# Split weights kept as single runs of 512 columns, and the first gate and up steps taken by halves

## The chip, the cores and the metric

The kernel runs on one core of a Trainium2 chip. The time is the device time of one execution in microseconds, as the median of several runs. One execution was also recorded by the hardware profiler; its page and trace are what is quoted as "the profile" and "the trace". In them PE is TensorE (matmuls), PEld its weight loads, DVE is VectorE, ACT is ScalarE, POOL is GpSimd and SP is SyncE, which here issues nearly all DMAs.

## What is computed

A two-layer encoder on a sequence of 256 rows of 1024 values. Each layer has a mixer with three groups of heads (neighbourhood attention, dilated window attention, grouped-query attention) and a gated feed-forward block. Weights and activations are float32.

```
def mixer_sublayer(x, ...):
    h = rms_norm(x, n1)
    proj = h @ w_in_l                       # 1024 x 2560
    ...                                     # three kinds of attention
    return x + mix @ w_out_l                # 1024 x 1024

def channel_sublayer(x, n2, w_gu, cw, cb, w_dn):
    h = rms_norm(x, n2)
    g, u = jnp.split(h @ w_gu, 2, axis=-1)  # 1024 x 5632
    g = depthwise_conv_centred(g, cw, cb)   # three taps along the rows
    return x + (jax.nn.gelu(g, approximate=False) * u) @ w_dn   # 2816 x 1024

for l in range(DEPTH):                      # DEPTH = 2
    x = mixer_sublayer(x, ...)
    x = channel_sublayer(x, ...)
```

The input is one batch of 256 x 1024 values; `D_FF` is 2816.

## The kernel before

**Split weights.** PE multiplies in fp32r. To keep float32 accuracy each weight and each activation is split into a high part (ACT casts it to fp32r, tile `wp_hi`) and a low part (DVE subtracts the high part from the original, tile `wp_lo`). Products of the two operands are then summed in up to three matmuls (`mm3`, line 595; in the gate and up steps two, since the activation's two parts lie side by side and go through one matmul of 512 columns).

**Units.** Weights are taken in units of at most 2048 columns (8 KB a partition), listed by `units_of` (line 530) in the order of use: twelve units of the input projections, six of the output projections (three or two chunks of 512), and for the feed-forward block `FFN` (line 69): G0, U0, G1, D0, U1, G2, D1, U2 and so on, where G, U and D are steps of gate, up and down. A gate or up unit is 8 input chunks by 256 columns, a down unit 2 chunks by 1024 columns. `load` (line 547) issues a unit's DMA into one of four raw buffers (tile `wp_raw`). `split` (line 569) makes the unit's two parts in places for two units: tags `hi` and `lo`, each a tile of 2048 columns in `PARTS` = 2 buffers. It works in pieces of about 512 columns, for a down unit 1024. A place comes free when the last matmul that reads the unit is done. `unit` (line 584) gives out the next unit; before that it puts into the program the loads up to four units and the splits up to `AHEAD` = 2 units, the one given out among them.

**The order of the work.** The program isn't issued as written. `Plan` (line 217) first collects all operations with their dependences, and `order` (line 298) lists them out by a cost model: of all operations that could start on their engines it takes the one with the earliest start, and among equal ones the one with the lowest rank. The rank is the place in the program, raised for some: the splits and loads by `SPLIT_LATER` = 50. Places of one tag are given in the order in which their tiles are first used in the program (`t.turn != s.given`), even where a later tile could use one sooner. So the place of a split in the program sets its rank and its turn, not its time.

**The passage from mixer to feed-forward block.** In lines 1206 to 1210 the last two output-projection units add to x; `split_T` (line 608) transposes half of x (input chunks 0 to 3) on PE and makes its high and low part (`h2`, in the trace `act_hT`) on ACT and DVE. `half_up` (line 1219) is a gate or up step: for each of two column groups j and each chunk k one matmul of 512 and one of 256 columns, 32 in all, into two banks of the pool `psw`. The first gate step takes chunks 0 to 3 of both groups, then makes the other half of `h2` with `split_T`, then takes chunks 4 to 7, and ends with `row_scale`.

`gate` (line 1264) copies and adds the two halves of each bank (`joined`, ACT and DVE), scales, applies the three taps (ACT, then DVE), and takes the gelu on ACT. `up` (line 1283) joins its banks, multiplies by the gelu's result and splits that into `act_ch` and `act_cl`. `down` (line 1293) multiplies these with a down unit into four banks `dacc` of the pool `psa`, which it holds through the block. The tiles of `joined`, of the taps and of the gelu share the tag `s2k` with five places.

The helper that issues every operation is line 402, so every row of the profile names line 402, and the rows are told apart by their tiles: `wp_hi`, `wp_lo` (split weights), `act_hT` (the normalised input), `psw` and `psa` (accumulators), `act_s2k` (gate and softmax work), `const_x` (x).

Of the kernel before, what the change touches and what calls it, by code (L numbers as in the profile page):

```python
# [11 lines left out]
F32 = mybir.dt.float32  # L12
# [6 lines left out]
P = 128  # L19
# [21 lines left out]

RAWS, PARTS, AHEAD, CHUNK = 4, 2, 2, 512

# [401 lines left out]
def encoder_kernel(  # L445
# [101 lines left out]
    def load(i):  # L547
# [19 lines left out]
        raws.append(raw)  # L567

    def split(i):
        v = views[i]  # L570
        a, b = v.shape[1], v.shape[2]
        n = a * b
        raw = raws[i]
        hi = wp.tile([P, UNIT], F32R, tag="hi", name=f"hi{i}", bufs=PARTS)
        lo = wp.tile([P, UNIT], F32R, tag="lo", name=f"lo{i}", bufs=PARTS)
        h = b if i < 2 else b * max(1, CHUNK // b)
        for c in range(0, n, h):
            e = min(c + h, n)
            nc.scalar.copy(hi[:, c:e], raw[:, c:e])
            nc.vector.tensor_tensor(lo[:, c:e], raw[:, c:e], hi[:, c:e].bitcast(F32), op=ALU.subtract)  # L580
        r = lambda z: z[:, :n].rearrange("p (a b) -> p a b", b=b)
        parts.append((r(hi), r(lo)))

    def unit():

        i = taken[0]
        taken[0] += 1
        with nc.later(SPLIT_LATER):
            while len(raws) < min(i + AHEAD + RAWS - PARTS, len(views)):
                load(len(raws))  # L590
            while len(parts) < min(i + AHEAD, len(views)):
                split(len(parts))
        return parts[i]
# [181 lines left out]
    for l in range(DEPTH):  # L775
# [9 lines left out]
        pj = {}  # L785

        def projections():
            for (c0, width), name in zip(PROJ, PROJ_NAMES):
                ps = [psa.tile([P, 512], F32, tag="a", name=f"pj_{name}{l}{t}") for t in range(NT)]
                per = 4 if width * 8 > UNIT else 8  # L790
                for k0 in range(0, KD, per):
                    wh, wl = unit()
                    for t in range(NT):
                        c = slice(t * P, (t + 1) * P)
                        for k in range(per):
                            kk = k0 + k
                            mm3(
                                ps[t][:, :width], hT_hi[:, kk, c], hT_lo[:, kk, c],
                                wh[:, k], wl[:, k], kk == 0, kk == KD - 1,
                            )  # L800
                            yield 3 * width / 2.4
                pj[name] = ps
                yield name
# [7 lines left out]
        def out_projections(order):  # L811
            for gi, h in order:
                k0, n = OUTP[gi]
                yield ("wait", f"mix{gi}")
                wh, wl = unit()
                for t in range(NT):
                    c = slice(t * P, (t + 1) * P)
                    ps = psa.tile([P, 512], F32, tag="a", name=f"po{gi}_{l}{t}_{h}")
                    for k in range(n):
                        kk = k0 + k  # L820
                        mm3(
                            ps, mixT_hi[:, kk, c], mixT_lo[:, kk, c], wh[:, k], wl[:, k], k == 0, k == n - 1
                        )
                        yield 3 * 512 / 2.4
# [393 lines left out]

        def half_up(name, first=False):

            wh, wl = unit()
            ps = [psw.tile([P, 2, S], F32, tag="w", name=f"{name}{j}") for j in range(2)]

            def part(j, k):
                js = slice(j * P, (j + 1) * P)
                nc.tensor.matmul(ps[j], wh[:, k, js], h2[:, k], start=k == 0, stop=False)
                nc.tensor.matmul(ps[j][:, 0], wl[:, k, js], h2_hi[:, k], start=False, stop=k == KD - 1)

            if first:
                for k in range(4):  # L1230
                    part(0, k)
                for k in range(4):
                    part(1, k)
                split_T(halves(1), h2_hi, h2_lo, 4, gains[:, 2, l, 4:8], f"n2{l}1")
                for k in range(4, KD):
                    part(0, k)
                for k in range(4, KD):
                    part(1, k)
                row_scale()
                return ps  # L1240
# [52 lines left out]
        def down(steps):  # L1293
            ws = [unit() for _ in steps]
            for h in range(2):
                hs = slice(h * 512, (h + 1) * 512)
                for t in range(NT):
                    c = slice(t * P, (t + 1) * P)
                    for s, (wh, wl) in zip(steps, ws):
                        ch, cl = ready[s]  # L1300
                        for j in range(2):
                            mm3(
                                dacc[t][h], ch[:, j, c], cl[:, j, c], wh[:, j, hs], wl[:, j, hs],
                                s == 0 and j == 0, s == STEPS - 1 and j == 1,
# [99 lines left out]
```

## Time and profile before

| | |
|---|---|
| median of 3 runs | 617.96 us (617.42 to 618.77) |
| the profiled execution | 618.73 us |
| its span, first to last instruction | 616.9 us |
| granted TensorE clock | 1.000 |
| DVE busy | 487.1 us (79%) |
| ACT busy | 429.8 us (70%) |
| HBM read | 102.54 MB |

A row of a timeline has the start from the span's beginning, the duration, the engine, the line, the operation, the tile written and the tiles read, the shapes, the count of merged instructions, and in brackets the idle time of the engine before it and what ended that. A row of a group has the count, the busy time, the mean of one in ns, and the idle time before. A row of stretches has start and end, then the busy time of each engine. Matmuls are pipelined and their ends are modelled, so a busy PE isn't PE at its peak.

### The profile page before, as it was taken

The page shows a single profiled execution, that of the slowest core. Times are in us where ns is not written, and L with a number is a line of the kernel's source. Part 1 is how long each engine was busy: PE and PEld are TensorE (multiplying, and loading weights), DVE is VectorE, ACT ScalarE, POOL GpSimd, SP SyncE. Part 2 cuts the span into 40 slices and gives each one's busy share as a digit, 9 for nine tenths or more (in the row PEclk, how much of TensorE's full clock was granted, in tenths as well). Part 3 has the DMA queues.
Part 4 walks back from the last instruction along what each step waited for, and adds up shares of the span by engine and source line. Part 5 has one row for each costly group of instructions (what it writes and reads, how often), then busy time and mean ns, then how long its engine had stood idle before and what let it go on. Part 6 is the DMA issues. An engine that isn't in the chain of part 4 may idle for free.

```text
span 616.9 us, 9838 instructions
## 1 busy us (share of the span) xinstructions
PE 607.5 (98%) x3496; PEld 525.4 (85%) x3496; DVE 487.1 (79%) x1000; ACT 429.8 (70%) x1064; POOL 78.1 (13%) x125
## 2 busy tenths in 40 slices
PE   8999999999999999999999999999999999999997
PEld 6998888878888888888899989887888888888885
DVE  4898888897878777777867798979877777787775
ACT  6888898777565565556588899897756566556651
POOL 2732130111600000000023212112000000000000
PEclk9999999999999999999999999999999999999999
DMA  8894303466596566554444632127575565556501
GB/s 276 270 285 163 104 34 105 143 218 198 195 225 224 176 201 204 198 169 162 154 147 151 232 104 86 35 73 247 181 236 172 188 206 192 166 189 203 178 29 68
DMA packets 81345, 104.66 MB, mean 170 GB/s; under 512 B 9464, under 2 KB 68952, under 8 KB 81296
## 3 DMA queue, kind: packets, MB, share of 16 engines
q1 hardware_dynamic: 80720, 103.51, 52.0%
q8 instruction: 27, 0.44, 0.3%
q10 hardware_dynamic: 576, 0.53, 0.3%
q14 instruction: 22, 0.18, 0.1%
HBM read 102.54 MB, written 1.49 MB: 169 GB/s over the span
## 4 chain that ended last, share of the span: by engine, by line
PE 93%; ACT 3%; DVE 2%; DMA 1%; issue 1%; ACTq 0%
PE psw_w L402 49%; PE psa_a L402 44%; ACT act_s2k L402 2%; DMA const_x<-in_x_dram 1%; DVE wp_lo L402 1%; DVE act_hT L402 1%; ACT act_ch L402 0%; DVE const_x L402 0%; ACTq L402 0%; ACT wp_hi L402 0%; DVE small_nm L402 0%; ACT act_mixT_hi L402 0%; DVE act_z L402 0%; ACT act_sqm L402 0%; DVE small_rs L402 0%
## 5 line engine op out<-in xcount | busy, mean ns | idle before, releaser
L402 DVE TENSOR_TENSOR wp_lo<-wp_raw,wp_hi 128x512 fp32r<-128x512 f32 (+2 forms) x348 | 244.5, 732 | 48.2 <-ACT wp_hi L402 46.3
L402 PE MATMUL psw_w<-act_hT,wp_hi 128*128 128x512 f32 x704 | 247.8, 397 | 2.7 <-DVE act_hT L402 2.7
L402 ACT CAST wp_hi<-wp_raw 128x512 fp32r<-128x512 f32 (+2 forms) x348 | 213.0, 659 | 25.0 <-PE psw_w L402 15.7
L402 PE MATMUL psw_w<-act_hT,wp_lo 128*128 128x256 f32 x704 | 195.8, 279 | 0.0
L402 PEld LDWEIGHTS psw_w<-act_hT,wp_hi 128*128 128x128 f32 x704 | 131.9, 188 | 35.1 <-DVE act_hT L402 3.9
L402 PEld LDWEIGHTS psw_w<-act_hT,wp_lo 128*128 128x128 f32 x704 | 132.6, 188 | 1.1
L402 PE MATMUL psa_a<-wp_hi,act_hT 128*128 128x384 f32 (+2 forms) x448 | 113.4, 333 | 0.0
L402 ACT COPY act_s2k<-psw_w 128x256 f32<-128x256 f32 x88 | 32.4, 373 | 80.5 <-PE psw_w L402 80.5
L402 PEld LDWEIGHTS psa_a<-wp_hi,act_hT 128*128 128x128 f32 x448 | 78.7, 190 | 2.4
L402 PE MATMUL psa_a<-wp_lo,act_hT 128*128 128x384 f32 (+2 forms) x224 | 75.0, 335 | 0.0
L402 PE MATMUL psa_a<-wp_lo,act_ch 128*128 128x512 f32 x176 | 69.5, 395 | 0.0
L402 PE MATMUL psa_a<-wp_hi,act_ch 128*128 128x512 f32 x176 | 69.3, 394 | 0.0
L402 PE MATMUL psa_a<-wp_hi,act_cl 128*128 128x512 f32 x176 | 66.1, 394 | 0.0
L402 DVE TENSOR_TENSOR act_s2k<-psw_w,act_s2k 128x256 f32<-128x256 f32 x88 | 36.8, 422 | 30.6 <-ACT act_s2k L402 30.2
L402 PEld LDWEIGHTS psa_a<-wp_lo,act_hT 128*128 128x128 f32 x224 | 42.4, 189 | 2.0 <-DVE wp_lo L402 1.1
L402 PEld LDWEIGHTS psa_a<-wp_hi,act_cl 128*128 128x128 f32 x176 | 33.1, 188 | 7.8
L402 PEld LDWEIGHTS psa_a<-wp_hi,act_ch 128*128 128x128 f32 x176 | 33.1, 188 | 7.8
L402 PEld LDWEIGHTS psa_a<-wp_lo,act_ch 128*128 128x128 f32 x176 | 33.1, 188 | 6.9
L402 DVE SCALAR_TENSOR_TENSOR act_s2k<-act_s2k,act_cw,act_s2k 128x255 f32<-128x255 f32 x88 | 36.8, 478 | 1.4 <-ACT act_s2k L402 1.3
L402 ACT ACTIVATE act_s2k<-act_s2k,act_cw 128x256 f32<-128x256 f32 x44 | 24.1, 595 | 11.6 <-DVE act_s2k L402 11.6
L402 POOL TENSOR_TENSOR small_rstd<-small_ms,const_mh 128x6 f32<-128x6 f32 (+2 forms) x26 | 31.5, 1210 | 2.1
L402 ACT ACTIVATE act_s2k<-act_s2k 128x512 f32<-128x512 f32 x22 | 13.9, 632 | 22.4 <-DVE act_s2k L402 22.4
(109 smaller groups left out, 773.3 us busy)
## 6 DMA issues: line engine op xcount, KB each, us to landing
wp_raw<-in_w_gate_up_dram SPq DMA_DIRECT2D x44, 1024.0 KB, 5.0
wp_raw<-in_w_down_dram SPq DMA_DIRECT2D x22, 1024.0 KB, 4.9
wp_raw<-in_w_in_dram SPq DMA_DIRECT2D x14, 768.0 KB, 5.7
wp_raw<-in_w_in_dram SPq DMA_DIRECT2D x8, 1024.0 KB, 5.8
wp_raw<-in_w_out_dram SPq DMA_DIRECT2D x8, 768.0 KB, 4.3
wp_raw<-in_w_out_dram SPq DMA_DIRECT2D x4, 512.0 KB, 3.7
act_nab<-dram_scr SPq DMA_DIRECT2D x4, 448.0 KB, 7.1
out_dram<-const_x SPq DMA_DIRECT2D x4, 256.0 KB, 2.0
```

Of the source, the lines that this page charges most:

```text
L402: getattr(o.engine.real, o.method)(*map(real, o.args), **{k: real(v) for k, v in o.kw.items()})
```

## The change

A unit's parts are no longer one tile of 2048 columns but single runs of at most 512, each with a place of its own: eight places a part (`PIECES`), as many bytes as before. `grain` says how a unit is cut: projections as before; a down unit into four runs (chunk by half of the columns) instead of two of 1024; a gate or up unit into four runs of four chunks by 128 columns, one column group at a time, instead of four runs of two chunks by 256. `AHEAD` becomes 3, so a split stands in the program one unit earlier; the loads stay at four units. The order of the matmuls in the projections and in all later steps stays as it was (`by_rows` is defined and not used).

`first_halves` joins the first gate step and the first up step of each layer: chunks 0 to 3 of G0, the other half of `h2`, chunks 0 to 3 of U0, chunks 4 to 7 of G0, `row_scale`, chunks 4 to 7 of U0. U0's two banks come from the pool `psa` there.

```diff
-RAWS, PARTS, AHEAD, CHUNK = 4, 2, 2, 512
+RAWS, PIECES, LOAD_AHEAD, AHEAD, CHUNK = 4, 8, 4, 3, 512
...
+    PER_LAYER = len(views) // DEPTH
+
+    def grain(i, a, b):
+
+        if b > CHUNK:
+            return 1, CHUNK
+        if i % PER_LAYER >= PER_LAYER - len(FFN):
+            return 4, P
+        return max(1, CHUNK // b), b
+
     def split(i):
         v = views[i]
         a, b = v.shape[1], v.shape[2]
         n = a * b
         raw = raws[i]
-        hi = wp.tile([P, UNIT], F32R, tag="hi", name=f"hi{i}", bufs=PARTS)
-        lo = wp.tile([P, UNIT], F32R, tag="lo", name=f"lo{i}", bufs=PARTS)
-        h = b if i < 2 else b * max(1, CHUNK // b)
-        for c in range(0, n, h):
-            e = min(c + h, n)
-            nc.scalar.copy(hi[:, c:e], raw[:, c:e])
-            nc.vector.tensor_tensor(lo[:, c:e], raw[:, c:e], hi[:, c:e].bitcast(F32), op=ALU.subtract)
-        r = lambda z: z[:, :n].rearrange("p (a b) -> p a b", b=b)
-        parts.append((r(hi), r(lo)))
+        rv = raw[:, :n].rearrange("p (a b) -> p a b", b=b)
+
+        per, w = (1, b) if i < 2 else grain(i, a, b)
+        cuts = [(k, c) for c in range(0, b, w) for k in range(0, a, per)]
+        both = {}
+        for k, c in cuts:
+            pair = [wp.tile([P, per, w], F32R, tag=g, name=f"{g}{i}_{k}_{c}", bufs=PIECES) for g in ("hi", "lo")]
+            src = rv[:, k : k + per, c : c + w]
+            nc.scalar.copy(pair[0], src)
+            nc.vector.tensor_tensor(pair[1], src, pair[0].bitcast(F32), op=ALU.subtract)
+            both[k // per, c // w] = pair
+        parts.append(lambda k, c=0, n=b: [z[:, k % per, c % w : c % w + n] for z in both[k // per, c // w]])
 
     def unit():
 ...
-            while len(raws) < min(i + AHEAD + RAWS - PARTS, len(views)):
+            while len(raws) < min(i + LOAD_AHEAD, len(views)):
                 load(len(raws))
             while len(parts) < min(i + AHEAD, len(views)):
                 split(len(parts))
...
-        def half_up(name, first=False):
...
+        def products(ps, w, j, ks):
+
+            for k in ks:
+                wh, wl = w(k, j * P, P)
+                nc.tensor.matmul(ps[j], wh, h2[:, k], start=k == 0, stop=False)
+                nc.tensor.matmul(ps[j][:, 0], wl, h2_hi[:, k], start=False, stop=k == KD - 1)
...
+        def half_up(name):
+            ps, w = banks(psw, "w", name), unit()
             for j in range(2):
-                for k in range(KD):
-                    part(j, k)
+                products(ps, w, j, range(KD))
             return ps
+
+        def first_halves():
+
+            G, U = banks(psw, "w", f"G{l}_0"), banks(psa, "a", f"U{l}_0")
+            wg = unit()
+            for j in range(2):
+                products(G, wg, j, range(4))
+            split_T(halves(1), h2_hi, h2_lo, 4, gains[:, 2, l, 4:8], f"n2{l}1")
+            wu = unit()
+            for j in range(2):
+                products(U, wu, j, range(4))
+            for j in range(2):
+                products(G, wg, j, range(4, KD))
+            row_scale()
+            for j in range(2):
+                products(U, wu, j, range(4, KD))
+            return G, U
...
         def gate(s):
             nm = f"{l}_{s}"
-            Gs = joined(half_up(f"G{nm}", s == 0), f"Gs{nm}")
+            if s == 0:
+                hold["G"], hold["U"] = first_halves()
+            Gs = joined(hold["G"] if s == 0 else half_up(f"G{nm}"), f"Gs{nm}")
...
         def up(s):
             nm = f"{l}_{s}"
-            C = joined(half_up(f"U{nm}"), f"C{nm}")
+            C = joined(hold["U"] if s == 0 else half_up(f"U{nm}"), f"C{nm}")
```

Elsewhere a unit's parts are taken by a call, `w(k)` or `w(j, h * 512, 512)`, where they were slices of one tile.

More of the change, by code (lines that the diff above doesn't have):

```diff
@@ L785, in encoder_kernel, with by_tiles, by_rows @@
         pj = {}
+        def by_tiles(n):
+            return [(t, k) for t in range(NT) for k in range(n)]
+        def by_rows(n):
+            return [(t, k) for k in range(n) for t in range(NT)]
         def projections():
@@ L1298, in down @@
                     c = slice(t * P, (t + 1) * P)
-                    for s, (wh, wl) in zip(steps, ws):
+                    for s, w in zip(steps, ws):
                         ch, cl = ready[s]
```

40 lines of the change are left out of this document (10 added, 30 removed).

## The prediction

> **What bounds the kernel now.** I read the page first: the span, the engines' busy time, and the idle time ahead of the feed-forward matmuls.
>
> ```profile
> span 616.9 us, 9838 instructions
> ...
> PE 607.5 (98%) x3496; PEld 525.4 (85%) x3496; DVE 487.1 (79%) x1000; ACT 429.8 (70%) x1064; POOL 78.1 (13%) x125
> ...
> L402 PE MATMUL psw_w<-act_hT,wp_hi 128*128 128x512 f32 x704 | 247.8, 397 | 2.7 <-DVE act_hT L402 2.7
> ```
>
> PE is busy for 607.5 of 616.9 us. The change adds and removes no matmul, so it can only move the 9.4 us in which PE is idle. 2.7 us of these stand in one group: gate and up matmuls that wait for the normalised input (act_hT). Then I cut the span into stretches of the first layer.
>
> ```profile
> core 0: us, PE busy (x) PEld busy (x) DVE busy (x) ACT busy (x) POOL busy (x), PEclk, DMA share, GB/s
> 100.60:114.30 13.70, 13.55 (x90) 11.27 (x88) 9.86 (x31) 13.63 (x38) 1.69 (x4) 1.00 0.24 81
> 124.10:130.50 6.40, 5.07 (x31) 4.31 (x31) 6.40 (x14) 5.96 (x15) 2.15 (x3) 1.00 0.63 223
> 130.50:143.80 13.30, 13.30 (x79) 11.69 (x79) 10.91 (x21) 9.79 (x17) 0.00 (x0) 1.00 0.54 183
> 233.27:249.94 16.67, 16.67 (x90) 14.23 (x89) 12.52 (x22) 9.97 (x19) 0.00 (x0) 1.00 0.56 188
> ```
>
> The last row is one steady step of gate, up and down: PE has no idle time, and neither DVE (12.52 of 16.67) nor ACT (9.97) is full. Nothing can be won there. The hole is in the second row: from 124.1 to 130.5 PE works 5.07 of 6.40 us while DVE is full. The timeline shows what stands there.
>
> ```profile
> 125.16 0.74 DVE L402 SCALAR_TENSOR_TENSOR const_x<-psa_a,small_rstd,const_x 128x512 f32<-128x512 f32 x1
> ...
> 125.81 3.09 DVE L402 TENSOR_TENSOR wp_lo<-wp_raw,wp_hi 128x512 fp32r<-128x512 f32 x5
> ...
> 126.91 0.91 PEld L402 LDWEIGHTS psw_w<-const_ident,const_x 128*128 128x128 f32 x8
> ...
> 128.85 1.66 DVE L402 SCALAR_TENSOR_TENSOR act_hT<-psw_w,const_gains,act_hT 128x256 fp32r<-128x256 f32 x4
> 129.39 0.19 PEld L402 LDWEIGHTS psw_w<-act_hT,wp_hi 128*128 128x128 f32 x1 [1.57 <-DVE act_hT L402]
> 129.39 0.50 PE L402 MATMUL psw_w<-act_hT,wp_hi 128*128 128x512 f32 x1 [1.33 <-DVE act_hT L402]
> ```
>
> PE has done the first half of G0 (gate step 0, input chunks 0 to 3) and the eight transposes of the second half, and then waits until DVE has written chunk 4: 1.33 us by the matmul, 1.57 us by its weight load. The 2.7 us of the group above are this place, once in each layer. The chain of waits gives the length of what follows.
>
> ```profile
> 129.39 14.38 PE psw_w L402 x82
> 143.77 5.56 PE psa_a L402 x24
> ```
>
> **The change part by part. First, the two half steps.** Between the transposes and G0's second half the change puts the first half of U0 (up step 0): 16 of the 80 feed-forward matmuls that now fill 14.38 us, so 16 x 14.38 / 82 = 2.8 us (the other two of the 82 are transposes). The wait is 1.33 to 1.57 us, so it is covered; chunk 4 stands at 129.3 and is now wanted at 127.8 + 2.8 = 130.6. PE is free for it at 129.39 - 1.57 = 127.8, and it needs the first run of U0's split weights then and the third 1.4 us later, at 129.2. Before, the five splits from 125.81 to 128.9 are G0's last two and U0's first three, in the same order, so even without any lead they come just in time, and in the stretch to 124 the finer places let some be done sooner. I take 1.5 us a layer, 3.0 us in all; bounds 0 (U0's runs late) and 3.1. U0's accumulators move to the other pool, where the out-projection's last bank is evicted by 125.9 (the row at 125.16): no wait. No DMA is added; loads stay four units ahead, and the step that issues U0's load moves ahead of 16 matmuls and the transposes, but SP issues by the freed raw buffer. Its cover is the load's lead:
>
> ```profile
> wp_raw<-in_w_gate_up_dram SPq DMA_DIRECT2D x44, 1024.0 KB, 5.0
> ```
>
> 5.0 us to land, issued at least two units (11 us) before use.
>
> **What is late next.** G0 now ends after U0's first half, 1.3 us later than before (2.8 less the 1.5 saved), while D0 (down step 0), the matmuls from 143.77, should start 1.5 us sooner. Between G0's end and D0 there are now U0 and G1, 64 matmuls, 11.3 us; after the change 48, 8.5 us. In this time the gate must be made and U0 multiplied in. Before, G0 ends at 143.8 - 11.3 = 132.4. This is what DVE and then ACT do until then:
>
> ```profile
> 133.06 0.68 DVE L402 TENSOR_TENSOR wp_lo<-wp_raw,wp_hi 128x512 fp32r<-128x512 f32 x1
> 133.65 0.42 DVE L402 TENSOR_TENSOR act_s2k<-psw_w,act_s2k 128x256 f32<-128x256 f32 x1
> 133.99 0.68 DVE L402 TENSOR_TENSOR wp_lo<-wp_raw,wp_hi 128x512 fp32r<-128x512 f32 x1
> 134.59 0.69 DVE L402 TENSOR_TENSOR act_s2k<-act_s2k,act_rb 128x512 f32<-128x512 f32 x1
> 135.19 1.29 DVE L402 TENSOR_TENSOR wp_lo<-wp_raw,wp_hi 128x512 fp32r<-128x512 f32 x2
> 136.39 1.67 DVE L402 SCALAR_TENSOR_TENSOR act_s2k<-act_s2k,act_cw,act_s2k 128x255 f32<-128x255 f32 x4
> ```
>
> ```profile
> 132.50 0.37 ACT L402 COPY act_s2k<-psw_w 128x256 f32<-128x256 f32 x1 [0.27 <-PE psw_w L402]
> 132.76 1.66 ACT L402 CAST wp_hi<-wp_raw 128x512 fp32r<-128x512 f32 x3
> 135.31 1.09 ACT L402 ACTIVATE act_s2k<-act_s2k,act_cw 128x256 f32<-128x256 f32 x2 [0.88 <-DVE act_s2k L402]
> ...
> 138.14 1.28 ACT L402 ACT_TABLE_LOAD   x1 [0.28 <-DVE act_s2k L402]
> 139.43 0.63 ACT L402 ACTIVATE act_s2k<-act_s2k 128x512 f32<-128x512 f32 x1
> 139.97 0.63 ACT L402 COPY act_s2k<-psw_w 128x256 f32<-128x256 f32 x2
> ...
> 141.87 0.62 ACT L402 CAST act_ch<-act_s2k 128x512 fp32r<-128x512 f32 x1
> ```
>
> D0's first operand (act_ch) is there at 142.49, 10.1 us after G0's end and 1.3 us before D0 starts. The same 10.1 us against 8.5 would make D0 late by 1.6 us, as much as was won. But three places of that chain are splits that DVE does in between: 0.6 us each ahead of the rows at 133.65 and 134.59, 0.35 us of the two at 135.19, so 1.5 us; without them it takes 8.6. U0's copies come behind the gelu in any case, since the places of these tiles are given in program order and the gelu's tile is earlier. The time lost at D0 is therefore between 0 (8.6 against 8.5) and 1.6 us a layer. After the change G1's and D0's splits become possible as single runs come free, and those issued three units ahead stand before the gate's chain in rank; against that, DVE's two 1024-element splits become shorter ones, and matmuls of U1 can be put in front of a late D0. I take 0.5, nearer the lower end: 1.0 us in both layers.
>
> [...]
>
> **Third, the finer runs.** Only the down weights are cut smaller: two runs of 1024 become four of 512, so 44 more casts and 44 more subtractions in 22 units. Gate and up keep 512 elements but read 128 of every 256.
>
> ```profile
> L402 DVE TENSOR_TENSOR wp_lo<-wp_raw,wp_hi 128x512 fp32r<-128x512 f32 x240 | 157.5, 687 | 16.1 <-ACT wp_hi L402 14.3
> ...
> L402 DVE TENSOR_TENSOR wp_lo<-wp_raw,wp_hi 128x1024 fp32r<-128x1024 f32 x44 | 54.1, 1233 | 28.2 <-ACT wp_hi L402 28.1
> ```
>
> An added subtraction costs 2 x 687 - 1233 = 141 ns, 44 of them 6.2 us of DVE, 0.28 us a step. A read in runs of 128 is in no row that I can compare, so I bound it: at no cost, and as if each of the three further runs cost the 141 ns of an instruction, 0.42 us a split, 3.4 us for a step's eight. DVE then works 12.52 + 0.28 + 3.4 = 16.2 of the step's 16.67 us: even the dear end is hidden behind PE, though barely, and with the cheap end 3.9 us are free. ACT has 6.7 us free. Cost on the path: 0; without the cover, 0.28 us a step, 6.2 us in all.
>
> [...]
>
> **Fourth, rank and places.** Splits now have the rank of one unit earlier, and a run's place is free as soon as PE has read that run. In projections and heads PE is nearly full and no matmul is added. What the order there gives or takes I can't see before; I bound it by the PE idle time outside the two holes: 9.4 - 2.7 = 6.7 us, part of it at the start and the end of the kernel, where nothing changes. An estimate from the first row of the stretches: 0.15 us of idle time in 13.70 is 2.7 us in the 250 us that are left of the span beside 22 steps of 16.67. That is the most to be won; for the loss see the third rival. I take a gain of 0.2, since the out-projection's short units (two and three runs) no longer hold a place for four.
>
> **The sum.** 3.0 - 1.0 + 0.2 = 2.2 us. The profiled execution took 618.73 us with a span of 616.9, 0.77 above the median of the runs, 617.96. A span of 614.7 goes with 616.5 us of that execution, and the median with 617.96 - 2.2 = 615.8 us.
>
> **The rivals.** *Given back at D0.* The chain of 10.1 us keeps its three splits, or meets others, since DVE works 10.91 of 13.30 us there: 1.6 us lost a layer against 1.5 won. For it: the splits of G1 and D0 now outrank the gate's chain. Against: fewer are left to do. Time 617.96 - 3.0 + 3.2 - 0.2, about 618.0.
>
> *Not what it says.* U0's third run isn't ready at 129.2, because DVE, full from 124.1 to 130.5, has no lead after all. PE then waits as before in another place: 617.6 to 618.3.
>
> *Slower: splits in the heads' ACT stretch.* From 100.6 to 114.3 ACT works 13.63 of 13.70 us on the last softmaxes, and after that PE has little but what hangs on them. With a higher rank and places freed run by run, casts that now fill ACT's later gaps can fall into this stretch. Each delays the last heads by its 0.52 us (the row at 132.76: three casts in 1.66 us, the last of them taking 0.62). Two a layer eat the 2.2 us; from the third on the kernel is slower; four a layer give 615.8 + 2 x 4 x 0.52 = 620.0 us. Against: there are places for as many split elements as before, and PE has out-projection matmuls to fill with.
>
> *More won.* The 2.7 us of idle time in the mixer and the 0.5 a layer at D0 all go: 615.8 + 0.2 - 2.7 - 1.0 = 612.3 us.
>
> **How the numbers follow.** Forecast 46%, own range 614.2 to 616.9; given back 18%; not what it says 4%; slower 22%; more won 10%. The range 613.0 to 620.2 leaves out the far part of the last two. 0.2% is 1.2 us, about what a measurement tells from no change. Faster by more: most of the forecast and more won, 54%. Within: given back, not what it says, and the edge of the forecast, 22%. Slower: the rest, 24%.
>
> **What would show it.** Right: U0 matmuls into the psa pool directly behind the transposes near 127.8, and no idle time <-DVE act_hT of over 0.3 us ahead of a gate matmul; D0's first matmul at about 142.7 with up to 0.5 us of idle time ahead of it; steady steps of 16.7 us; 44 more weight casts, and none of 1024 elements. The second part is wrong if D0 waits 1.6 us or none; the third if a steady step grows: 0.1 us in each of twenty steps is 2 us. The forecast falls if the stretch from 60 to 117 us becomes longer by more than 1 us.

## The result, and the profile after

The changed kernel takes 625.12 us (median of 4 runs, 623.85 to 626.54), the kernel before on the same chip 618.37 us. The ratio is 1.0111, 95% interval 1.0097 to 1.0125: slower by 6.8 us, where 2.2 us less were forecast. The profiled execution took 625.81 us, its span is 7.1 us longer. The page of the changed kernel, its head and some groups:

```profile
span 624.0 us, 10138 instructions
...
PE 609.7 (98%) x3496; PEld 527.7 (85%) x3496; DVE 496.2 (80%) x1044; ACT 440.2 (71%) x1108; POOL 81.8 (13%) x125
...
L402 ACT CAST wp_hi<-wp_raw 128x512 fp32r<-128x512 f32 (+1 forms) x392 | 231.3, 608 | 129.6 <-PE psw_w L402 77.6
...
L402 PE MATMUL psw_w<-act_hT,wp_hi 128*128 128x512 f32 x672 | 237.7, 398 | 1.4 <-DVE act_hT L402 1.4
...
L402 PE MATMUL psa_a<-wp_hi,act_ch 128*128 128x512 f32 x176 | 69.4, 395 | 2.2 <-ACT act_ch L402 2.2
```

PE has as many matmuls as before. The group that waited 2.7 us for act_hT waits 1.4, and down matmuls, which had no such wait, now wait 2.2 us for act_ch. The stretches show the steady step as before, and something the prediction has nowhere, two rows with a granted clock of 0.50:

```profile
126.56:129.97 3.41, 2.89 (x8) 2.46 (x9) 3.41 (x8) 1.58 (x6) 1.75 (x1) 0.50 0.15 49
...
233.27:249.94 16.67, 16.67 (x90) 14.22 (x89) 12.94 (x23) 10.36 (x21) 0.00 (x0) 1.00 0.57 189
392.80:396.21 3.41, 3.41 (x14) 2.94 (x14) 3.04 (x9) 3.10 (x10) 1.44 (x2) 0.50 0.00 0
```

The timeline of PE where the first layer passes from mixer to feed-forward, first in the kernel before (last head matmul, transposes of the first half, last output-projection matmul, first gate matmul, transposes of the second half), then in the changed one (last head matmul, last output-projection matmul, transposes, G0, transposes, U0):

```profile
115.74 0.28 PE L402 MATMUL psw_w<-act_ch,const_v 128*128 128x256 f32 x1
...
121.49 0.38 PE L402 MATMUL psw_w<-const_ident,const_x 128*128 128x128 f32 x2
...
122.17 0.82 PE L402 MATMUL psw_w<-const_ident,const_x 128*128 128x128 f32 x6
...
123.76 0.40 PE L402 MATMUL psa_a<-wp_hi,act_mixT_lo 128*128 128x512 f32 x1
124.12 0.50 PE L402 MATMUL psw_w<-act_hT,wp_hi 128*128 128x512 f32 x1
...
127.03 1.03 PE L402 MATMUL psw_w<-const_ident,const_x 128*128 128x128 f32 x8
```

```profile
118.25 0.28 PE L402 MATMUL psw_w<-act_ch,const_v 128*128 128x256 f32 x1
...
123.06 0.39 PE L402 MATMUL psa_a<-wp_hi,act_mixT_lo 128*128 128x512 f32 x1
124.11 0.44 PE L402 MATMUL psw_w<-const_ident,const_x 128*128 128x128 f32 x2 [0.67 <-DVE const_x L402]
124.77 0.87 PE L402 MATMUL psw_w<-const_ident,const_x 128*128 128x128 f32 x6 [0.22 <-DVE const_x L402]
127.08 0.79 PE L402 MATMUL psw_w<-act_hT,wp_hi 128*128 128x512 f32 x1 [1.43 <-DVE act_hT L402]
...
131.31 1.04 PE L402 MATMUL psw_w<-const_ident,const_x 128*128 128x128 f32 x8
132.10 0.48 PE L402 MATMUL psa_a<-act_hT,wp_hi 128*128 128x512 f32 x1
```

The half steps are there: U0's matmuls into psa stand behind the second transposes, and no wait follows. But the last head is 2.5 us later. Before, the transposes of the first half (121.49 and 122.17) stood among the last output-projection matmuls; now the output projections end before the transposes can begin, and PE has three pauses (0.67, 0.22, 1.43 us) ahead of G0's first half. Then G0's first half runs from 127.08 to 131.31, 4.23 us against 2.91 before, up to 129.97 at the granted clock of 0.50. Next, D0 in the first layer, on POOL, DVE and PE:

```profile
147.36 1.83 POOL L402 COPY act_nab<-act_few 28x1984 f32<-28x1984 f32 x1 [16.24 <-DMA act_few<-in_rpb_dram]
147.37 0.41 DVE L402 TENSOR_TENSOR act_s2k<-psw_w,act_s2k 128x256 f32<-128x256 f32 x1
147.71 2.04 DVE L402 TENSOR_TENSOR act_s2k<-act_s2k,act_s2k 128x512 f32<-128x512 f32 x1
...
150.45 0.50 PE L402 MATMUL psa_a<-wp_hi,act_ch 128*128 128x512 f32 x1 [1.75 <-ACT act_ch L402]
```

The product of gate and up, which DVE makes for D0, takes 2.04 us beside a GpSimd copy that prepares the next layer's table; its like take 0.69. PE waits 1.75 us. In the second layer, without such a copy, the wait is 0.5 us. The second layer's mixer has a pause of its own, in front of the turning of a softmax, and the low clock of 392.80 follows it:

```profile
392.12 0.65 PE L402 MATMUL psw_w<-const_ident,act_s2k 128*128 128x128 f32 x4 [1.90 <-ACT act_s2k L402]
```

From the starts of the first projection matmul, of the first gate matmul and of D1's first matmul in the two timelines the 7.1 us can be laid out. This table gives the same for the kernels of the experiments (profiled executions, us):

| kernel | projections to G0, layer 1 | layer 2 | G0 to D1, layer 1 | layer 2 |
|---|---|---|---|---|
| before | 116.06 | 112.56 | 36.35 | 36.36 |
| changed | 119.19 | 115.66 | 38.86 | 35.67 |
| fine_rank2 | 119.61 | 114.45 | 36.05 | 36.06 |
| fine_rank2_halves | 118.77 | 114.46 | 35.20 | 35.33 |
| mix_whole | 117.41 | 113.35 | 36.25 | 36.18 |
| mix_whole_halves | 116.53 | 113.08 | 37.29 | 35.87 |
| mix_whole_halves_na | 117.05 | 113.10 | 35.66 | 35.67 |
| mix_whole_halves_gelu | 116.88 | 113.14 | 35.00 | 34.99 |
| fine_proj_na | 116.11 | 112.55 | 35.54 | 36.09 |
| fine_outproj_na | 117.06 | 113.47 | 36.89 | 35.19 |
| after_na_later | 118.77 | 115.63 | 35.28 | 35.69 |
| after_na_gelu | 118.26 | 115.90 | 34.72 | 35.02 |

The two mixers lose 3.13 and 3.10 us, the first feed-forward start loses 2.51, the second gains 0.69, and the rest of the span gains 0.95: together 7.1. PE's rows of the two mixers, before and then changed, show what kind of time the mixers lose:

```profile
8.06:124.12 116.06, 115.45 (x762) 1.00 0.55 169
313.12:425.68 112.56, 112.36 (x742) 1.00 0.39 127
```

```profile
7.89:127.08 119.19, 115.92 (x762) 0.99 0.59 180
318.13:433.79 115.66, 113.76 (x746) 0.99 0.43 141
```

PE's idle time grows by 2.7 and 1.7 us, its busy time by 0.5 and 1.4 us, at nearly the same matmuls and a lower clock. In the first layer the three pauses ahead of G0 make 2.3 us of the idle time, in the second the pause ahead of the softmax 1.9.

### The profile page after: what moved, and what is told of

Read it like the earlier page. It is cut to its first block, busy times and chain, and to the rows that moved or that the text cites. A ratio compares the mean times of both kernels' runs of the same rounds, so it can differ in the third digit from the quotient of the medians.

```text
span 624.0 us, 10138 instructions
## 1 busy us (share of the span) xinstructions
PE 609.7 (98%) x3496; PEld 527.7 (85%) x3496; DVE 496.2 (80%) x1044; ACT 440.2 (71%) x1108; POOL 81.8 (13%) x125
## 4 chain that ended last, share of the span: by engine, by line
PE 91%; DVE 3%; ACT 2%; POOL 1%; DMA 1%; issue 1%; ACTq 0%; DVEq 0%; POOLq 0%
PE psw_w L402 48%; PE psa_a L402 44%; DVE wp_lo L402 1%; ACT act_s2k L402 1%; DMA const_x<-in_x_dram 1%; POOL small_rstd L402 1%; DVE act_s2k L402 1%; ACT L402 0%; DVE const_x L402 0%; ACT wp_hi L402 0%; POOL small_ms L402 0%; DVE act_z L402 0%; DVE small_nm L402 0%; ACTq L402 0%; POOL act_sdq L402 0%
## 5 line engine op out<-in xcount | busy, mean ns | idle before, releaser
L402 ACT CAST wp_hi<-wp_raw 128x512 fp32r<-128x512 f32 (+1 forms) x392 | 231.3, 608 | 129.6 <-PE psw_w L402 77.6
L402 DVE TENSOR_TENSOR wp_lo<-wp_raw,wp_hi 128x512 fp32r<-128x512 f32 (+1 forms) x392 | 258.0, 674 | 77.2 <-ACT wp_hi L402 76.2
L402 PE MATMUL psw_w<-act_hT,wp_hi 128*128 128x512 f32 x672 | 237.7, 398 | 1.4 <-DVE act_hT L402 1.4
L402 PE MATMUL psw_w<-act_hT,wp_lo 128*128 128x256 f32 x672 | 187.7, 280 | 0.0
L402 PEld LDWEIGHTS psw_w<-act_hT,wp_hi 128*128 128x128 f32 x672 | 126.6, 189 | 32.3 <-DVE act_hT L402 2.1
L402 PEld LDWEIGHTS psw_w<-act_hT,wp_lo 128*128 128x128 f32 x672 | 127.2, 189 | 1.0
L402 PE MATMUL psa_a<-wp_hi,act_cl 128*128 128x512 f32 x176 | 68.9, 395 | 0.2 <-DVE act_cl L402 0.2
L402 DVE TENSOR_TENSOR act_s2k<-psw_w,act_s2k 128x256 f32<-128x256 f32 x84 | 34.8, 417 | 0.1
L402 PE MATMUL psw_w<-act_ch,const_v 128*128 128x256 f32 x128 | 29.5, 291 | 0.1
L402 ACT ACTIVATE act_s2k<-act_s2k,small_rs 128x256 f32<-128x256 f32 x64 | 28.6, 509 | 0.2
```

The costliest lines, as they stand in the source:

```text
L402: getattr(o.engine.real, o.method)(*map(real, o.args), **{k: real(v) for k, v in o.kw.items()})
```

## The experiments

**Which part costs.** Four kernels share their runs of the kernel before, 618.8 us. They take the three parts (half steps, finer places, three units ahead) in turn.

`unit_halves`: the kernel before with `first_halves`; whole-unit places, two units ahead.

```diff
-            Gs = joined(half_up(f"G{nm}", s == 0), f"Gs{nm}")
+            if s == 0:
+                hold["G"], hold["U"] = first_halves()
+            Gs = joined(hold["G"] if s == 0 else half_up(f"G{nm}"), f"Gs{nm}")
```

> The kernel before with the two half steps alone: places for whole units, two units ahead. Theory 1 (the loss comes from the splits of the mixer, which delay the last heads; the half steps are about even): G0 begins near 124 us as before, no drop of the granted clock there, the wait of 1.3 us ahead of G0's second half is gone, D0 waits 0 to 1.6 us; 616 to 618.5 us. Theory 2 (the loss comes from the half steps themselves, D0 late and the clock dropped): over 620 us.

Measured: 625.41 us, ratio 1.0109 (1.0089 to 1.0129): the time is theory 2's, the cause is in neither. The list of PE's waits (total, times, longest) says why:

```profile
PE psw_w L402 <- ACT wp_hi L402: 3.3, 2, 1.7
PE psw_w L402 <- DVE wp_lo L402: 2.5, 2, 1.9
```

G0's place comes free only after its second half, now 2.9 us later, and G1's weights, which take that place, come late in both layers. With two whole-unit places the half steps cost more than they gain.

`fine_rank3` (the changed kernel without half steps) and `fine_rank2` (that, two units ahead):

```diff
-RAWS, PIECES, LOAD_AHEAD, AHEAD, CHUNK = 4, 8, 4, 3, 512
+RAWS, PIECES, LOAD_AHEAD, AHEAD, CHUNK = 4, 8, 4, 2, 512
```

> The changed kernel without the half steps: single runs, three units ahead, gate step 0 by halves and up step 0 whole as before. Theory 1: the last heads end 2 to 3 us later than before in both mixers, G0 begins near 127 us, the clock drops in the wait; 623 to 627 us. Theory 2: 617.5 to 619 us, G0 near 124.

> As the one before, but splits two units ahead as in the kernel before; only the places are finer. If the rank of the splits (three ahead) delays the heads: 617 to 619 us. If it is the places, which let splits start earlier whatever their rank: 622 to 627 us.

Measured: 622.65 us, 1.0063 (1.0045 to 1.0081), and 622.73 us, 1.0057 (1.0040 to 1.0074). The first is just under theory 1's range, the second in the range given for the places. The finer places cost about 4 us by themselves, whatever the rank, and for `fine_rank2` the table puts it in the mixers.

`fine_rank2_halves`: the changed kernel, two units ahead.

> The changed kernel with splits two units ahead. If the rank is the cause: 615 to 618.5 us. If the places are: 623 to 627 us. With the two above it also shows what the half steps are worth on finer places: theory 1 within 2 us of the run without them, theory 2 at least 3 us slower.

Measured: 620.06 us, 1.0031 (1.0012 to 1.0050), between the two expected ranges. On finer places the half steps gain 2.7 us by the medians and 1.6 by the ratios, whose intervals overlap. With the half steps the third unit ahead costs 5 us (625.12 against 620.06), where without them it costs nothing. The PE waits of `fine_rank2_halves`:

```profile
PE psw_w L402 <- DVE act_hT L402: 3.2, 2, 1.6
...
PE psa_a L402 <- ACT act_ch L402: 0.7, 2, 0.4
```

D0 waits 0.4 us a layer, and the pause for act_hT stands ahead of G0's first half in both layers.

**Is it the mixer's places, and what is wrong at D0?** `mix_whole` gives the mixer's weights whole-unit places again: in the planner one tile takes four neighbouring runs of the same eight, so the feed-forward keeps its finer places and no storage is added. No half steps, two units ahead. `mix_whole_halves` has the half steps too.

```diff
+        if i % PER_LAYER < PER_LAYER - len(FFN):
+            hi, lo = [wp.tile([P, UNIT], F32R, tag=g, name=f"{g}{i}", bufs=PIECES) for g in ("hi", "lo")]
+            hi.tile.wide = lo.tile.wide = 4
...
+            return
```

> The kernel before with finer places for the feed-forward weights alone: the weights of the projections and output projections keep whole-unit places (two, as before), two units are split ahead, and there are no half steps. Theory (the finer places in the mixer delay its last heads, the rest of the 4 us): the mixer of the first layer is again instruction for instruction that of before, its first gate matmul starts at 124.1 +- 0.3 us of the span, and the time is that of before, 618.4 +- 0.7 us. Rival (finer places cost something wherever they stand, through more splits or earlier transfers): 620 us or more, as in the two kernels with finer places throughout (622.7).

Measured: 619.40 us, 1.0004 (0.9993 to 1.0014): the time of the kernel before, whose own median was 619.12 in these runs. The profiled execution, the slowest of 12, started its projections 0.8 us late and has G0 at 126.29, not at 124.1; from the first projection matmul to G0 it takes 1.35 us more than the kernel before, where `fine_rank2` takes 3.55 more. All of the 1.35 us arise in the first 18 us of the projections. Up to G0 in the first layer its trace has PE's matmuls in the order of the kernel before, every one of 749 (those on the constant tile `const_warm` left out), and so have all traces here with whole-unit places in the mixer. In the changed kernel the order differs from 30 us behind the first projection matmul on, and 443 of the 749 stand in the same position.

> As the run with whole places in the mixer and finer ones in the feed-forward alone, and with the two half steps. Theory (half steps gain 2 to 3 us once their weights have finer places; the mixer was what lost): the mixer of the first layer ends as before, first gate matmul at 124.1 +- 0.3, no wait of 1.3 us ahead of the second half of G0, D0 late by about 0.5 us a layer, 615.8 us (615.0 to 616.8): faster than before and than the change. Rival (half steps themselves cost, by the collision at D0 or by pauses that bring the clock down): 618.4 us or more.

Measured: 619.20 us, 1.0003 (0.9994 to 1.0013); no gain and no loss. The theory missed; the time is the rival's. The table shows the gain in the second layer and a loss of 0.94 us in the first. The timeline there:

```profile
145.40 1.83 POOL L419 COPY act_nab<-act_few 28x1984 f32<-28x1984 f32 x1 [16.10 <-DMA act_few<-in_rpb_dram]
...
145.59 2.19 DVE L419 TENSOR_TENSOR act_cl<-act_s2k,act_ch 128x512 fp32r<-128x512 f32 x1
...
147.83 0.50 PE L419 MATMUL psa_a<-wp_hi,act_cl 128*128 128x512 f32 x1 [1.19 <-DVE act_cl L419]
```

The same copy, here beside the subtraction for D0's low part: the collision at D0 that the rival names. Two cures were tried. `mix_whole_halves_gelu` issues a gelu of one column behind the mixer's last ScalarE work; `after_na_later` moves the next layer's table work in the changed kernel, and `mix_whole_halves_na` does so here.

```diff
+        early = small.tile([P, 1], F32, tag="early", name=f"early{l}", bufs=2)
+        with nc.not_before("ACT"):
+            nc.scalar.activation(early, ones, AF.Gelu)
```

```diff
-        NA_STEPS = {2: na_load, 3: na_repeat, 4: na_diagonals}
+        NA_STEPS = {4: na_load, 5: na_repeat, 6: na_diagonals}
...
-            if kind == "G" and l + 1 < DEPTH and s == 4:
+            if kind == "G" and l + 1 < DEPTH and s == 6:
```

> As the run before it, and with a gelu of one column issued after the mixer's last ScalarE instruction, so that the load of the gelu table (1.28 us in the first layer's gate chain) is done before G0 ends. Theory (the gate chain with the table load is what makes D0 late by 0.5 us a layer): D0's wait falls to under 0.2 us in both layers, 0.5 to 1.0 us less than the run before it, about 615 us. Rival (the load only moves and delays the first feed-forward splits or the splits of h2): same time as the run before it, within 0.3 us, or longer.

Measured: 616.26 us, 0.9952 (0.9939 to 0.9964): faster than both kernels, by 2.9 us than before, and more than the 0.5 to 1.0 us expected, since the wait of 1.19 us for the low part goes too. The table load stands in the mixer now, D0's first operand is ready early, and D0 starts without a wait:

```profile
115.23 1.28 ACT L419 ACT_TABLE_LOAD   x1
116.53 0.20 ACT L419 ACTIVATE small_early<-const_ones 128x1 f32<-128x1 f32 x1
...
144.20 0.62 ACT L419 CAST act_ch<-act_s2k 128x512 fp32r<-128x512 f32 x1
```

```profile
145.32 0.40 PE L419 MATMUL psa_a<-wp_hi,act_ch 128*128 128x512 f32 x1
...
145.81 2.03 POOL L419 COPY act_nab<-act_few 28x1984 f32<-28x1984 f32 x1 [16.07 <-DMA act_few<-in_rpb_dram]
```

The copy is still there, but D0's subtraction is over when it starts. The steps from G0 to D1 take 35.0 us in both layers, 1.36 less than before.

> The changed kernel with the next layer's table work (its load, the GpSimd copy, the diagonals, the tables) put two feed-forward steps later, so that the GpSimd copy of 1.83 us no longer runs at D0 of the first layer. Theory (the copy stretches the VectorE subtract that D0 waits for from 0.69 to 2.04 us): the subtract beside D0 is back at about 0.7 us, D0's wait in the first layer falls from 1.75 to about 0.5 us, and the time by 1.3 us or more, to 622.5 - 624 us. Rival (the subtract is slow for another reason, the copy is only beside it): D0's wait stays above 1.5 us and the time at 625.1 +- 0.7 us.

Measured: 622.48 us, 1.0052 (1.0040 to 1.0064), 3.7 us less than the changed kernel by the ratios. D0's waits are 0.5 and 0.4 us. That is more than the 1.35 us of the operation that DVE makes beside the copy (a product, not a subtraction): the mean granted clocks are higher (0.995 to 0.997 against 0.989 to 0.995; 0.997 against 0.992 in the profiled executions), and G0 to D1 of the first layer is shorter by 3.58 us.

> The kernel with whole places in the mixer, finer ones in the feed-forward and the two half steps, with the next layer's table work two feed-forward steps later. In the profile before this edit the GpSimd copy of the table ran from 145.40 to 147.23 us, beside the VectorE subtract that makes the second half of D0's input, which took 2.19 us where it takes 0.69 elsewhere, and PE waited 1.2 us for it in the first layer. Theory (the collision took back what the half steps gained): that subtract takes 0.7 us, the wait of 1.2 us is gone, the time falls by 1.0 to 1.5 us, to 617.5 - 618.3 us, just faster than before. Rival (half steps gain nothing here anyway): within 0.4 us of 619.2 us.

Measured: 618.19 us, 0.9989 (0.9979 to 0.9998), as expected. DVE's subtraction:

```profile
145.72 0.68 DVE L419 TENSOR_TENSOR act_cl<-act_s2k,act_ch 128x512 fp32r<-128x512 f32 x1
```

**What in the mixer.** `fine_proj_na` and `fine_outproj_na` are `mix_whole_halves_na` with finer places for the projections' weights alone, or for the output projections' alone (the condition of the edit above names the other units).

> As the run before it, but the projections' weights too live in the finer places; those of the output projections keep whole-unit places. It parts the mixer's loss: from the first projection matmul to the first gate matmul the first layer took 116.1 us in the kernel before and 119.2 in the changed one. Theory A (splits of output-projection and first feed-forward weights pulled in between the last heads delay them, 11 weight casts from 100 to 120 us where there were 8): this run keeps 116.1 to 117.0 us and the time of the run before it, within 0.5 us. Theory B (earlier splits of the projections' weights set another order of the heads from the start): 118.5 us or more, and 2 to 4 us slower than the run before it.

> The other part: the output projections' weights in finer places, those of the projections in whole ones. Theory A (pulled-in splits delay the last heads): 118.5 us or more from the first projection matmul to the first gate matmul in the first layer, and 2 to 4 us slower than the run with both whole. Theory B (the projections' order): 116.1 to 117.0 us, and the time of the run with both whole within 0.5 us.

Measured: 617.11 us, 0.9969 (0.9957 to 0.9981), and 620.19 us, 1.0017 (1.0007 to 1.0028). By time theory A holds: the output projections' places cost about 2 us, the projections' none (the kernel is 1.1 us faster). By the mixers' length neither does: 117.06 us with the finer output-projection places, 117.05 without. The weight casts on ACT from 85 to 120 us (busy time and count, then clock, DMA share and GB/s), in the order before, changed, `fine_outproj_na`:

```profile
85.00:120.00 35.00, 7.60 (x14) 1.00 0.24 78
```

```profile
85.00:120.00 35.00, 9.79 (x17) 1.00 0.35 109
```

```profile
85.00:120.00 35.00, 10.51 (x19) 1.00 0.38 124
```

With five more casts among the heads than before, more than in the changed kernel, the last head comes 108.2 us after the first projection matmul (before 107.7, changed 110.4). So the number of pulled-in casts isn't what delays the heads. What costs in `fine_outproj_na` is seen on PE, and in its row of stretches:

```profile
121.76 0.40 PE L419 MATMUL psa_a<-wp_hi,act_mixT_lo 128*128 128x512 f32 x1
...
122.77 0.88 PE L419 MATMUL psw_w<-const_ident,const_x 128*128 128x128 f32 x6 [0.22 <-DVE const_x L419]
125.08 0.80 PE L419 MATMUL psw_w<-act_hT,wp_hi 128*128 128x512 f32 x1 [1.43 <-DVE act_hT L419]
```

```profile
124.84:128.25 3.41, 3.17 (x10) 2.69 (x11) 2.56 (x6) 1.81 (x6) 1.83 (x3) 0.54 0.00 0
```

Weights that are ready sooner let PE finish the output projections sooner (last one at 121.76, where it was 123.76 before), and then nothing is left to cover the transposes and h2's first splits. The pause that the half steps fill at G0's second half stands at its first half, and the clock falls: the last row has a mean of 0.54, and if it is 0.50 where it is low, about 3.1 of these 3.41 us are low (an estimate from that row).

`fine_outproj_na_fill` adds 12 idle matmuls a layer there, on a tile of ones, into a bank that nothing reads:

```diff
+        fp = psa.tile([P, 512], F32, tag="a", name=f"fill{l}")
+        with nc.not_before("PE"):
+            for _ in range(12):
+                nc.tensor.matmul(fp[:, :WARM_W].rearrange("p (a b) -> p a b", b=P), warm, ...)
```

> The kernel with finer places for the output projections' and the feed-forward's weights, half steps and the table work later, and 12 idle matmuls (128x256, bf16, into a psum place that nothing reads) in each layer behind the last output-projection matmul, so that PE keeps working in the pause ahead of G0's first half. Without them that pause was 1.4 us (behind 0.7 us of shorter ones), the granted clock fell to 0.50 for 3.41 us at 124.84 us, and 10 of 11 timed executions had a mean granted clock of 0.994 to 0.997 and 619.65 to 620.81 us, the other 1.0 and 617.84 us. Theory (the pause brings the clock down, and the low clock costs 1.7 to 2 us): with the pause filled the clock stays at 1.0 through the first layer's G0, most executions show 1.0, and the median falls to 617.8 - 618.4 us. Rival (the clock falls for another reason, or the loss is the pause itself): 619.5 us or more.

Measured: 619.05 us, 0.9998 (0.9988 to 1.0008). Eight of 12 executions have a mean clock of 1.0, where it was one of 11, and the median falls by 1.1 us:

```profile
124.15 1.25 PE L419 MATMUL psa_a<-const_warm 128*128 128x256 bf16 x10
125.74 0.50 PE L419 MATMUL psw_w<-act_hT,wp_hi 128*128 128x512 f32 x1 [0.34 <-DVE act_hT L419]
```

```profile
125.74:129.15 3.41, 3.41 (x20) 2.86 (x21) 3.02 (x6) 2.39 (x7) 2.09 (x3) 1.00 0.03 4
```

The clock falls here with the pause and not without it, as the theory has it (0.54 from 124.84 to 128.25 us without the idle matmuls, 1.00 from 125.74 to 129.15 with them), but the time lies between the two expectations, so filling the pause is worth about 1 us here, not 2.

**Three units ahead, and the rest.** `mix_whole_halves_gelu_rank3` issues the feed-forward's splits three units ahead:

```diff
-            while len(parts) < min(i + AHEAD, len(views)):
+            while len(parts) < min(i + AHEAD + (i % PER_LAYER >= PER_LAYER - len(FFN)), len(views)):
```

> The fastest kernel so far (whole places in the mixer, finer ones in the feed-forward, half steps, the early gelu: 616.3 us) with the splits of the feed-forward's weights issued three units ahead instead of two. Theory (the third unit ahead is worth nothing in the feed-forward, where PE waits for no weights): the same time within 0.6 us and steady steps of 16.7 us. Rival (the third unit's splits get in the way of the gate chain or of the activations of D0): a wait at D0 of 0.5 us or more comes back in one layer or both, 617 us or more.

Measured: 617.69 us, 0.9981 (0.9972 to 0.9989), slower by 0.0029 of the kernel before than with two. Its waits contain 0.6 us of U0's first half for act_hT and 0.2 us at D0 for act_cl, which two units ahead has not: the time is the rival's, the wait at D0 smaller than the 0.5 us that it named.

`after_na_gelu` has both cures in the changed kernel, and `fine_proj_gelu` is `fine_proj_na` with the early gelu in place of the later table work.

> The changed kernel with both cures at D0: the next layer's table work two steps later and the early gelu. What is left of its loss is then the mixer's and the clock's. Theory (D0's waits of 0.4 to 0.5 us a layer go, the mixer with finer places throughout keeps its 2 to 3 us a layer and its drops of the clock): 621.0 to 622.0 us, still slower than before by 2 to 3 us and than the same with whole places in the mixer (616.3 us) by about 5. Rival (the loss sat in the feed-forward): at or under 619 us.

Measured: 622.96 us, 1.0051 (1.0033 to 1.0070), 1 us above the expectation and no better than `after_na_later`. D0's waits are gone (G0 to D1 is 34.72 and 35.02 us), but four of seven executions have a mean clock of 0.988 to 0.992 and take 622.96 to 624.87 us; the other three, at 0.997, take 620.87 to 621.49. The mixers keep their loss, 2.2 and 3.3 us.

> Finer places for the projections' and the feed-forward's weights, whole ones for the output projections, half steps, and the early gelu instead of the later table work. Theory (D0's waits of 0.5 us a layer go, nothing else changes): 616.0 to 616.4 us, at least as fast as the fastest so far (616.26 us). Rival (the early gelu changes the planner's order of the last heads): 617 us or more.

Measured: 616.93 us, 0.9960 (0.9945 to 0.9976), between the two expected ranges: no D0 wait, the same as the fastest kernel within the intervals.

## Why the prediction was wrong

**First, the two half steps: right.** U0's first half is in place and takes 2.9 us (132.10 to 135.00; forecast 2.8), and the wait ahead of G0's second half is gone in both layers. On the same places the half steps with D0's wait gained 1.6 us by the ratios, 2.7 by the medians (`fine_rank2` to `fine_rank2_halves`; forecast 3.0 - 1.0 = 2.0).

**What is late next: right in the second layer, too small in the first.** D0 waits 0.5 us in the second layer, the value taken. That the chain with the table load is what makes it late is shown by the early gelu, which takes the wait away in both layers. In the first layer it was 1.75 us, over the bound of 1.6, since DVE's product within the chain took 2.04 us instead of 0.69 beside the table's copy of 1.83 us. The prediction counted what DVE and ACT do between G0 and D0 and left POOL out. Before the change the copy ran at 152.66, clear of the chain. It waits for its DMA, which SP issued at 147.79 before, behind 31 loads of weights, and at 142.75 after, behind 30: the planner lists it one weight load sooner. `fine_rank2_halves` has 31 again, and its copy runs at 153.1. The prediction had only said of SP that it issues by the freed raw buffer.

**Third, the finer runs: right.** 392 casts, none of 1024 elements; the steady step is 16.67 us with DVE at 12.94 (12.52 before, 12.80 at the cheap end of the forecast). In the feed-forward alone the finer places cost nothing (`mix_whole`, ratio 1.0004).

**Fourth, rank and places: this step failed.** It took a gain of 0.2 us in the mixer, at most 2.7, and no loss beside the third rival. The two mixers lost 6.2 us of the 7.1. With whole-unit places there, all else kept (`fine_rank2` to `mix_whole`), the time is back at that of before, and so is the order of PE's matmuls in the first layer. So the finer places in the mixer are the cause of the loss of about 4 us that they bring alone. The rank adds nothing to that without the half steps, but about 5 us with them; `after_na_later`, which moves the table's copy away from D0, takes back 3.7. The premise "no matmul is added and PE is nearly full" holds; but it left out that the planner lists another order when splits can start at other times, and that PE being full depended on that order: the last output projections covered the way to G0, and in the changed kernel and in `fine_outproj_na` they are done before the transposes can begin.

**The third rival had the sign, not the mechanism.** It gave 620.0 us by casts among the last heads. There were such casts, and `fine_outproj_na` has even more of them, with the last head 0.55 us later instead of 2.7.

**What no part had: the clock.** A pause of 1.4 to 1.9 us was counted at its own length. In the profile of the changed kernel the clock falls at two such pauses, of 1.43 and 1.90 us, to 0.50 for 3.41 us, and a third place of low clock stands at the start; by the mean clocks the four executions have two to four places each (an estimate: 3.41 us at half clock are 0.0027 of the span's mean). In the first layer the low clock costs 1.3 us in G0's first half (4.23 us against 2.91). In the second, `fine_rank3` has the same order of PE's matmuls up to G0 and the same pause of 1.9 us, but no low clock behind it (its mean clock of 0.997 is one place by this estimate, and that one touches the stretch from 124.54 to 127.95 us, with 0.99): counted from the first projection matmul, the changed kernel is 0.05 us behind it ahead of that place and 1.6 us after it. In `fine_rank2_halves` the executions with a mean clock of 0.999 take 618.43 and 619.02 us, those of 0.997 take 619.95 to 620.21, those of 0.994 take 622.34 to 623.47. The change of rank belongs here too: with the half steps, three units ahead (625.12 us) against two (620.06) brought the copy beside D0 and more places of low clock (mean clocks of 0.989 to 0.995 against 0.994 to 0.999).

**Open.** In the profiles of the kernels with both the projections' and the output projections' weights in finer places the last heads come 1.3 to 3.7 us later behind the first projection matmul than before. In the first layer this distance differs by up to 1.4 us also between kernels that have PE's order of before, all of it in the first 18 us. Counted from there the last head of the first layer comes 1.8 to 3.3 us later with both, 0.3 to 0.6 with either alone, and at the same time with neither. The order of the work of ACT and DVE differs from the projections on; which of the exchanges delays the heads was not tried.

## What to carry to other kernels

An order that a planner lists is part of what a profile shows: an edit that only frees buffers sooner can change it everywhere, so confine such an edit to the stage where the profile shows the wait. Here the finer places in the feed-forward alone, two units ahead, took 619.2 us instead of 625.1, and 616.3 with the gelu's table loaded early. When work is moved ahead of a wait, look at what else covers that wait's inputs, and at every engine with an instruction in the chain's new window, POOL and its DMA included. A short pause of PE in a stage that it bounds can cost more than its length: here the clock fell to 0.50 for 3.41 us at one of 1.43 us, and G0's first half took 4.23 us instead of 2.91.

## What the runs showed of the hardware

**The low clock of the changed kernel stands on a grid.** There the granted clock falls to 0.50 at 7.10, 126.56 and 392.80 us (to about 0.02 us), each time for 3.41 us (the first at the start of the kernel, right behind a wait of PE of 0.74 us for x); the distances are 119.46 and 266.24 us, 35.0 and 78.0 times this length (3.413 us by the trace). What PE did in the 3.41 us ahead of the two later ones:

```profile
123.15:126.56 3.41, 1.61 (x10) 1.00 0.81 259
389.39:392.80 3.41, 1.51 (x18) 1.00 0.00 0
```

It was busy for less than half of each stretch, for 1.61 and 1.51 us, without one pause longer than 1.9 us. The busy time doesn't settle it alone: from 147.04 to 150.45 us of the changed kernel, six lengths of the grid behind 126.56, PE is busy for 1.66 us, and the clock stays at 1.00 behind it, while in `fine_outproj_na` it falls near 125.1 us (the estimate from the mean of 0.54), behind 3.41 us in which PE is busy for about 1.8 us (added up from its timeline's rows). So no threshold is shown. Nor is it shown where the pauses of other executions lie on this grid, and whether the spread of one kernel's times comes from that.

**Two VectorE operations beside a GpSimd copy took three times as long, a third did not.** The product at 147.71 in the changed kernel takes 2.04 us beside the copy, the subtraction at 145.59 in `mix_whole_halves` 2.19. The product ends at 149.75, 0.56 us after the copy's end at 149.19; the subtraction at 147.78, 0.55 after its copy. Both end about as if they had waited for the copy's end and then done most of the 0.69 us that such an operation takes elsewhere (an estimate from these ends); with the copy moved away the subtraction takes 0.68 us (`mix_whole_halves_na`). The sum at 147.37, which has one of its inputs in an accumulator (psw), runs beside the same copy in 0.41 us, its usual time. What sets the operations apart was not tried.
